# A kernel that orders its own instructions: another charge for TensorE's matmuls in its clock, and some transposes in another order

## The chip, the cores and the metric

The kernel runs on one core of one Trainium2 chip. The metric is the device time of one execution in microseconds, the median over several runs. The names of the engines are those of the profile: PE is TensorE (its matmuls), PEld the loading of its stationary operand, DVE is VectorE, ACT is ScalarE, POOL is GpSimd, SP is SyncE, which issues the weight transfers.

## The reference

The reference is a decoder trunk of two layers over x of 512 positions by 1024 channels, in float32.

```
for l in range(2):
    h = rmsnorm(x)
    p = h @ w_in[l]                          # 1024 -> 3328, split over four mixers
    y = rwkv7(p0), stick_breaking(p1), retention(p2), conformer_conv(p3)   # each 512 x 256
    merged = sum_i sigmoid(h @ w_gate[l, i]) * (y[i] @ w_branch[l, i])
    x = x + merged @ w_out[l]
    h = rmsnorm(x)
    x = x + (swiglu(h) if l == 0 else top2_of_8_experts(h))
```

The RWKV-7 mixer is a recurrence with a 64 x 64 state per head, done here in 8 chunks of 64 positions. The stick-breaking mixer is a causal attention whose logarithms of weights are running sums along the keys. The dense feed-forward part has width 2816. In the last part each of the 512 positions goes to 2 of 8 experts of width 1408.

## The kernel before, in words

**Products.** Every large product is made from three matmuls in the type fp32r: weight and input are each split into a high and a low part, and high x high, high x low and low x high are added up in PSUM. In the trace these are the matmuls that read whi, wlo (two layers) or mhi, mlo, hw (experts). ACT writes the high part of a weight, DVE the low part. The mixers' own small products, and all transposes, are matmuls in float32 (PSUM tile mx, some in po).

**Order.** The program is laid out by Python code that carries a clock of its own (class Clock): for each instruction that is issued it adds a charge to that engine's time, and holds for each stretch of a tile when it will be written and read. The instructions of each engine run in the order in which the code issues them; what the clock says decides nothing but that order. The stream of large matmuls is the backbone. After every six of them (two blocks of three) `group` calls `slot`, and `slot` calls `pump`. `pump` goes through the generators that are under way (rwkv, sb and sb_chunk, ret, conv, norm, moe_put, moe_prep) and lets one go a step further when two conditions hold: its `ready` time is not after PE's time on the clock, and DVE's and ACT's times are not ahead of PE's by more than a limit (LIMS). After a step, `ready` is the time at which all that the step issued will be done, plus 100 ns, or PE's time plus the number of ns that the generator asks for (`yield 6000.0`), whichever is later. So the code puts the small matmuls of a mixer into the backbone where, by its clock, their inputs have been ready for at least 100 ns.

**Charges.** `mm` charges a matmul in fp32r n / 2.4 ns for n columns out (120 ns if n is under 192), one in float32 n / 0.6 ns; `tr` charges a transpose 107 ns. `Engine.cost` charges DVE 69 + 1.042 n and ACT 94 + 0.833 n for most operations. DVE's running sum (tensor_tensor_scan) is charged like any other operation.

**Experts.** The eight expert positions are worked off in the order 4, 0, 5, 1, 6, 2, 3, 7 (PORD). Positions 0 and 1 have room for 160 rows, 2 and 3 for 144, the others for 128 (CAP). While one position is worked, `moe_prep` prepares the next: it builds a one-hot matrix, gathers the rows with an indirect DMA (an index per row), waits 16000 ns of the clock, scales the rows (ACT), waits 6000 ns, then transposes them with PE and splits the result into the tile hw (ACT the high part, DVE the low part). For the larger positions there are two sets of rows: 128, and 32 or 16. For each of the 8 blocks of 128 channels there are then two transposes, one of a 128 x 128 block and one of a 32 x 128 (16 x 128) block. In the trace they are the PE rows of line 478 with mx<-cst,f, with forms 128\*128 128x128 and 32\*128 32x32 (16\*128 16x16).

The lines to know: 473 (the charge in `mm`), 478 (`tr`), 474 (all other matmuls), 214 (all ACT, DVE and POOL operations: `Engine.__getattr__`), 371 (loads of ACT's tables).

Of the kernel before, what the change touches and what calls it, by code (L numbers as in the profile page):

```python
# [10 lines left out]
R = mybir.dt.float32r  # L11
# [8 lines left out]
KC = D // 128  # L20
# [12 lines left out]
CAP = [128 + OV] * 2 + [128 + OV // 2] * 2 + [128] * 4  # L33
# [286 lines left out]
class Trunk:  # L320
# [148 lines left out]
    def mm(self, out, lhsT, rhs, start=True, stop=True):  # L469
        n = 1  # L470
        for d in out.shape[1:]:
            n *= d
        self.clock.run("pe", max(n / 2.4, 120.0 if n < 192 else 27.0) if lhsT.dtype == R else max(n / 0.6, 105.0), [out], [lhsT, rhs])
        self.nc.tensor.matmul(out, lhsT, rhs, start=start, stop=stop)  # L474

    def tr(self, out, in_, ident):
# [31 lines left out]

    def rwkv(self, out):
        m, mm, v, g, a = self.m, self.mm, self.v, self.g, self.a  # L510
        P = self.rwp
        ident, bones = self.c("ident"), self.c("bones")
# [9 lines left out]
        for j in range(2):  # L522
            sl = slice(j * 128, (j + 1) * 128)
            ps = self.ps()
            mm(ps, self.lora[0:64, 0, sl], tw[0:64])
            t = m(S)
            a(t[:], ps, AF.Sigmoid, bias=self.p("w0", j))
            sig.append(t)
            ps = self.ps()
            mm(ps, self.lora[64:128, 0, sl], P[6][64:128])  # L530
            t = m(S)
            a(t[:], ps, AF.Sigmoid, bias=self.p("a0", j))
            aa.append(t)
            if j == 0:
                yield
# [1351 lines left out]
    def moe_prep(self, p, put):  # L1887

        slots = []
        O = self.moe_O(self.moe_new, self.rkp[:, :, p], CAP[p])  # L1890
        yield 5000.0
        self.moe_slots(self.moe_new, O, self.V[:, :, p, :], CAP[p], slots)
        yield 16000.0
        if len(slots) == 1:
            H = [self.mt(n, [128, KC, 128], R) for n in ("hh", "hl")]
            for k0 in (0, 4):
                self.moe_T(slots[0][2][:, k0 * 128:], 4, 128, H[0][:, k0:], H[1][:, k0:])
                yield
        else:
            H = [self.mt("hw", [128, KC, 2, 128 + OV], R, 2)[:, :, :, 0:CAP[p]]]  # L1900
            for _, v, xg, m in slots:
                self.a(xg[0:m], xg[0:m], AF.Identity, scale=v[0:m, 2:3])
            yield 6000.0
            for k0 in range(0, KC, 2):
                ps = self.ps(shape=(128, 2, CAP[p]))
                for k in range(2):
                    for i, (_, _, xg, m) in enumerate(slots):
                        self.tr(ps[:, k, 128 * i:128 * i + m], xg[0:m, (k0 + k) * 128:(k0 + k + 1) * 128],
                                self.c("ident")[0:m, 0:m])
                self.split(H[0][:, k0:k0 + 2, 0], H[0][:, k0:k0 + 2, 1], ps)  # L1910
                if k0 % 4 == 2:
                    yield
        put.append((slots, H))

    def moe_up(self, H, g, r, todo, ks):
# [278 lines left out]
```

## Time and profile before

| | |
|---|---|
| median of 3 runs | 1893.22 us (1893.21 to 1894.51) |
| the profiled execution's own time | 1892.88 us |
| its span, from first to last instruction | 1891.0 us |
| PE busy | 1865.9 us, 99% of the span |
| PEld, DVE, ACT, POOL busy | 1518.9, 1258.0, 970.4, 131.1 us |
| granted TensorE clock | 0.997 of full speed |

Matmuls are pipelined, so that one's duration (say 393 ns) is longer than the distance to the next one's start; what a matmul costs the stream is read from starts. The layers' stages lie so: the first layer's mixers from the start to about 425 us, the dense part to 880 us, the second layer's mixers to about 1360 us, the routing and the first expert's start to 1420 us, the experts to the end.

### The profile page before, as it was taken

What the parts mean: (1) busy time and instruction counts of PE and PEld (TensorE: products, weight loads), DVE (VectorE), ACT (ScalarE), POOL (GpSimd) and SP (SyncE); (2) the same over time, 40 slices, a digit from 0 to 9 for tenths busy, and PEclk for the clock granted to TensorE, in tenths of its full rate; (3) what the DMA queues carried; (4) which work ended last, traced back from release to release, by engine and by line L of the source; (5) the groups of instructions that cost most, each with busy time, mean ns of one, the idle gap of its engine ahead of it and who ended that gap; (6) DMA issues with size and microseconds to landing.
All of it is one profiled execution on the core that took longest, in us unless ns stands there. A gap on an engine that the chain in (4) does not pass through costs nothing. (4 is left out here: it accounts for less than half of the span.)

```text
span 1891.0 us, 26090 instructions
## 1 busy us (share of the span) xinstructions
PE 1865.9 (99%) x10028; PEld 1518.9 (80%) x10028; DVE 1258.0 (67%) x1978; ACT 970.4 (51%) x1427; POOL 131.1 (7%) x184
## 2 busy tenths in 40 slices
PE   8999999999999999999999999999999999999998
PEld 6777777678888888888777877778879889789886
DVE  6779875754663333346778886664578787787776
ACT  5653555743543232235553435674467576676664
POOL 1001100000000000001001100010111011110100
PEclk9999999999999999999999999999999999999999
DMA  5222321132323223224222321133379788798876
GB/s 194 101 79 79 95 79 56 56 128 84 122 101 99 90 101 100 91 91 168 101 78 67 107 89 56 67 118 117 123 303 354 274 320 288 267 346 268 266 247 224
DMA packets 110818, 283.46 MB, mean 150 GB/s; under 512 B 8816, under 2 KB 59632, under 8 KB 102752
## 3 DMA queue, kind: packets, MB, share of 16 engines
q1 hardware_dynamic: 101472, 254.03, 38.5%
q0 software_dynamic: 9072, 27.68, 5.1%
q8 instruction: 81, 1.33, 0.3%
q14 instruction: 49, 0.40, 0.1%
q10 hardware_dynamic: 144, 0.02, 0.0%
HBM read 265.84 MB, written 13.76 MB: 148 GB/s over the span
## 5 line engine op out<-in xcount | busy, mean ns | idle before, releaser
L474 PE MATMUL mm<-s,whi 128*128 128x512 f32 x3168 | 1000.4, 397 | 9.2 <-ACT whi L214 5.8
L474 PEld LDWEIGHTS mm<-s,whi 128*128 128x128 f32 x3168 | 587.4, 188 | 147.4 <-issue 14.2
L474 PE MATMUL mm<-s,wlo 128*128 128x512 f32 x1584 | 619.0, 391 | 0.0
L214 ACT ACTIVATE whi<-wraw 128x512 fp32r<-128x512 f32 (+1 forms) x432 | 261.1, 620 | 212.9 <-PE mm L474 128.1
L214 DVE TENSOR_TENSOR wlo<-wraw,whi 128x512 fp32r<-128x512 f32 (+1 forms) x432 | 286.8, 681 | 123.4 <-ACT whi L214 122.6
L474 PEld LDWEIGHTS mm<-s,wlo 128*128 128x128 f32 x1584 | 298.0, 188 | 64.1 <-DVE wlo L214 0.6
L214 DVE TENSOR_TENSOR mlo<-mraw,mhi 128x2048 fp32r<-128x2048 f32 (+2 forms) x146 | 300.8, 2080 | 25.3 <-ACT mhi L214 25.3
L214 ACT ACTIVATE mhi<-mraw 128x2048 fp32r<-128x2048 f32 (+2 forms) x146 | 253.9, 1750 | 66.8 <-PE po L474 30.6
L214 ACT ACTIVATE s<-s 128x512 f32<-128x512 f32 (+3 forms) x238 | 150.0, 658 | 182.5 <-DVE s L214 180.4
L214 DVE TENSOR_TENSOR s<-s,s 128x512 f32<-128x512 f32 (+19 forms) x369 | 216.2, 593 | 37.4 <-ACT s L214 27.0
L214 ACT ACTIVATE s<-mm 128x512 f32<-128x512 f32 x108 | 64.1, 594 | 214.7 <-PE mm L474 206.5
L214 DVE TENSOR_TENSOR s<-s,mm 128x512 f32<-128x512 f32 x91 | 62.1, 685 | 137.6 <-PE mm L474 111.3
L474 PE MATMUL mm<-mhi,g 128*128 128x512 f32 x352 | 99.5, 393 | 0.0
L474 PEld LDWEIGHTS mm<-mhi,g 128*128 128x128 f32 x352 | 65.4, 188 | 18.4
L214 DVE SCALAR_TENSOR_TENSOR s<-s,par,s 128x512 f32<-128x512 f32 (+31 forms) x110 | 77.5, 733 | 0.4
L474 PE MATMUL mm<-mhi,hh 128*128 128x512 f32 (+1 forms) x192 | 72.4, 377 | 0.0
L474 PE MATMUL mm<-mhi,hl 128*128 128x512 f32 (+1 forms) x192 | 71.5, 372 | 0.0
L214 ACT ACTIVATE s<-mx 128x512 f32<-128x512 f32 (+3 forms) x83 | 39.8, 512 | 54.0 <-PE mx L474 26.5
L474 PE MATMUL mm<-hw,mhi 128*128 128x320 f32 (+1 forms) x384 | 63.8, 306 | 0.0
L474 PEld LDWEIGHTS mx<-s,s 64*64 64x64 f32 (+3 forms) x752 | 41.9, 145 | 21.6 <-issue 13.7
L474 PE MATMUL mm<-mlo,g 128*128 128x512 f32 x176 | 58.7, 392 | 0.0
L371 ACT ACT_TABLE_LOAD x44 | 56.5, 1283 | 0.7
(188 smaller groups left out, 1866.7 us busy)
## 6 DMA issues: line engine op xcount, KB each, us to landing
mraw<-moe_w_d SPq DMA_DIRECT2D x102, 1024.0 KB, 7.0
wraw<-w_gate_d SPq DMA_DIRECT2D x64, 512.0 KB, 3.5
wraw<-ffn_w_d SPq DMA_DIRECT2D x60, 512.0 KB, 3.5
wraw<-w_in_d SPq DMA_DIRECT2D x51, 512.0 KB, 3.5
mraw<-moe_w_d SPq DMA_DIRECT2D x32, 768.0 KB, 6.2
wraw<-w_branch_d SPq DMA_DIRECT2D x32, 256.0 KB, 2.6
mraw<-moe_w_d SPq DMA_DIRECT2D x12, 512.0 KB, 6.0
wraw<-w_out_d SPq DMA_DIRECT2D x10, 512.0 KB, 4.3
```

Of the source, the lines that this page charges most:

```text
L214: return f(out, *a, **k)
L371: self.nc.scalar.preload_act_table_set(want)
L474: self.nc.tensor.matmul(out, lhsT, rhs, start=start, stop=stop)
```

## The change

In `mm` the charge of an fp32r matmul becomes n / 2.4 + 13.7 ns instead of n / 2.4, and the lower bound for n under 192 becomes 109 ns instead of 120. No other charge is touched. For 512 columns that is 227.0 instead of 213.3 ns, for 320 columns 147.0 instead of 133.3, for 288 columns 133.7 instead of 120, for 160 and 144 columns 109 instead of 120.

In `moe_prep`, for the larger positions, the transposes of four channel blocks at a time go into two PSUM tiles: first the four of the 128 rows, then the four of the 32 or 16 rows, and the two splits follow. Before, one PSUM tile held two channel blocks, the two forms took turns, and each tile's split was issued right behind it. There is a `yield` after each four channel blocks, before and after.

```diff
-        self.clock.run("pe", max(n / 2.4, 120.0 if n < 192 else 27.0) if lhsT.dtype == R else max(n / 0.6, 105.0), [out], [lhsT, rhs])
+        self.clock.run("pe", max(n / 2.4 + 13.7, 109.0 if n < 192 else 27.0) if lhsT.dtype == R else max(n / 0.6, 105.0), [out], [lhsT, rhs])
...
-            for k0 in range(0, KC, 2):
-                ps = self.ps(shape=(128, 2, CAP[p]))
-                for k in range(2):
-                    for i, (_, _, xg, m) in enumerate(slots):
-                        self.tr(ps[:, k, 128 * i:128 * i + m], xg[0:m, (k0 + k) * 128:(k0 + k + 1) * 128],
-                                self.c("ident")[0:m, 0:m])
-                self.split(H[0][:, k0:k0 + 2, 0], H[0][:, k0:k0 + 2, 1], ps)
-                if k0 % 4 == 2:
-                    yield
+            for k0 in (0, 4):
+                ps = [self.ps(shape=(128, 2, CAP[p])) for _ in range(2)]
+                for i, (_, _, xg, m) in enumerate(slots):
+                    for k in range(4):
+                        self.tr(ps[k // 2][:, k % 2, 128 * i:128 * i + m],
+                                xg[0:m, (k0 + k) * 128:(k0 + k + 1) * 128], self.c("ident")[0:m, 0:m])
+                for k in (0, 2):
+                    self.split(H[0][:, k0 + k:k0 + k + 2, 0], H[0][:, k0 + k:k0 + k + 2, 1], ps[k // 2])
+                yield
```

## Rows read from the trace of the kernel before

**Rows 1.** The page's first two parts: busy time, share and instructions of each engine, and the granted clock in 40 slices, in tenths.

```profile
PE 1865.9 (99%) x10028; PEld 1518.9 (80%) x10028; DVE 1258.0 (67%) x1978; ACT 970.4 (51%) x1427; POOL 131.1 (7%) x184
...
PEclk9999999999999999999999999999999999999999
```

**Rows 2.** The table of windows, rows for six of the stages: start and end, length, then busy us and instructions of PE, PEld, DVE, ACT, POOL, the granted clock, the DMA engines' share and GB/s.

```profile
15.00:210.00 195.00, 195.00 (x978) 156.23 (x977) 160.91 (x299) 98.05 (x168) 17.39 (x32) 1.00 0.29 96
210.00:425.00 215.00, 209.19 (x1292) 155.50 (x1291) 144.11 (x261) 119.04 (x191) 8.66 (x18) 0.99 0.24 82
425.00:880.00 455.00, 455.00 (x2020) 376.92 (x2019) 212.11 (x338) 162.30 (x276) 11.96 (x28) 1.00 0.31 104
...
1120.00:1310.00 190.00, 188.93 (x1051) 140.79 (x1050) 112.97 (x199) 112.00 (x180) 8.11 (x14) 1.00 0.27 91
1360.00:1420.00 60.00, 57.15 (x338) 48.55 (x337) 41.45 (x90) 34.85 (x39) 10.31 (x11) 1.00 0.74 279
1420.00:1882.00 462.00, 461.73 (x2772) 401.97 (x2771) 354.36 (x386) 305.05 (x343) 44.29 (x24) 1.00 0.85 289
```

**Rows 3.** The waits of PE over the whole span: who waited for whom, us in total, times, the longest. Five of its nine rows; the others are small or lie in the mixers (rows 13).

```profile
PE mm L474 <- ACT whi L214: 5.8, 1, 5.8
...
PE mx L478 <- ACT s L214: 2.4, 4, 0.9
PE mx L474 <- DVE uv L214: 1.4, 2, 0.9
...
PE po L474 <- DVE f L214: 0.8, 1, 0.8
PE mm L474 <- DVE mlo L214: 0.6, 2, 0.4
```

**Rows 4.** The table of windows (columns as in rows 2) for a stretch in the dense part that holds nothing but fp32r matmuls of 512 columns on PE.

```profile
600.00:800.00 200.00, 200.00 (x884) 165.62 (x883) 72.49 (x112) 57.34 (x95) 0.00 (x0) 1.00 0.29 97
```

**Rows 5.** The timeline of PE in an expert with 160 rows (start, length of the run, engine, line, operation, tiles, form of the first, count): eight transposes in turns of the two forms, and the large matmul behind them; then the page's grouping by form of the same eight.

```profile
1549.02 1.75 PE L478 MATMUL mx<-cst,f 128*128 128x128 f32 x8
1550.70 2.12 PE L474 MATMUL mm<-mhi,g 128*128 128x512 f32 x8
...
L478 PE MATMUL mx<-cst,f 128*128 128x128 f32 x4 | 1.3, 314 | 0.0
L478 PE MATMUL mx<-cst,f 32*128 32x32 f32 x4 | 1.0, 244 | 0.0
```

**Rows 6.** The same timeline for a position with 144 rows.

```profile
1672.96 1.70 PE L478 MATMUL mx<-cst,f 128*128 128x128 f32 x8
1674.58 0.73 PE L474 MATMUL mm<-mhi,g 128*128 128x512 f32 x2
```

**Rows 7.** The timeline of PE where eight, and where four, transposes of one form stand together (in the brackets the idle time before).

```profile
379.17 1.09 PE L478 MATMUL mx<-cst,s 128*128 128x128 f32 x8 [0.95 <-ACT s L214]
380.02 0.71 PE L474 MATMUL mm<-s,whi 128*128 128x512 f32 x2
...
1469.65 0.60 PE L478 MATMUL mx<-cst,f 128*128 128x128 f32 x4
1470.00 1.27 PE L474 MATMUL mm<-hw,mhi 128*128 128x320 f32 x7
```

**Rows 8.** The groups by form of PE from 1420 us to the end: all transposes of the small forms in the kernel.

```profile
L478 PE MATMUL mx<-cst,f 32*128 32x32 f32 x16 | 3.9, 244 | 0.0
L478 PE MATMUL mx<-cst,f 16*128 16x16 f32 x16 | 3.7, 231 | 0.0
```

**Rows 9.** The timeline of PE around two other runs of one small form: 64 matmuls with 32 columns in the stationary operand, and 8 with 128 columns in it and 4 columns out.

```profile
225.15 2.11 PE L474 MATMUL mx<-s,f 32*32 32x32 f32 x64
227.19 0.66 PE L478 MATMUL mx<-cst,s 128*128 128x128 f32 x4
...
1452.25 0.95 PE L474 MATMUL mx<-V,O 128*128 128x4 f32 x8
1453.06 1.12 PE L474 MATMUL mm<-hw,mhi 128*128 128x320 f32 x6
```

**Rows 10.** The timeline of DVE and of PE before the transposes of rows 5: the last weights' low parts that DVE made, and the matmuls that read them.

```profile
1541.10 3.42 DVE L214 TENSOR_TENSOR mlo<-mraw,mhi 128x1536 fp32r<-128x1536 f32 x2
...
1551.40 0.88 DVE L214 TENSOR_TENSOR hw<-mx,hw 128x320 fp32r<-128x320 f32 x2
...
1548.33 0.86 PE L474 MATMUL mm<-mlo,hh 128*128 128x384 f32 x4
```

**Rows 11.** The groups by form of DVE from 15 to 1310 us: the running sums.

```profile
L214 DVE TENSOR_TENSOR_SCAN s<-s,s 128x512 f32<-128x512 f32 x12 | 14.2, 1212 | 0.2 <-ACT s L214 0.2
L214 DVE TENSOR_TENSOR_SCAN s<-s,s 128x384 f32<-128x384 f32 x8 | 7.5, 944 | 1.4 <-ACT s L214 1.4
...
L214 DVE TENSOR_TENSOR_SCAN s<-s,s 128x128 f32<-128x128 f32 x8 | 3.2, 400 | 0.0
```

**Rows 12.** The timeline of DVE and of PE around the longest wait of PE in the mixers.

```profile
329.25 2.33 DVE L214 TENSOR_TENSOR_SCAN s<-s,s 128x512 f32<-128x512 f32 x2
331.61 1.83 DVE L214 TENSOR_TENSOR s<-s,s 128x1024 f32<-128x1024 f32 x2
...
335.39 0.68 DVE L214 TENSOR_TENSOR s<-s,mm 128x512 f32<-128x512 f32 x1
...
333.35 0.39 PE L474 MATMUL mm<-s,wlo 128*128 128x512 f32 x1
336.13 0.73 PE L474 MATMUL mm<-s,whi 128*128 128x512 f32 x2 [2.39 <-DVE s L214]
```

**Rows 13.** The waits of PE in the two stages with mixers alone (15 to 440 us, four rows; then 900 to 1360 us, the first of three).

```profile
PE mm L474 <- DVE s L214: 2.4, 1, 2.4
PE mx L478 <- ACT s L214: 2.2, 3, 0.9
PE mx L474 <- ACT s L214: 0.8, 1, 0.8
PE mx L474 <- ACT f L214: 0.4, 1, 0.4
...
PE mm L474 <- DVE s L214: 0.6, 1, 0.6
```

## The prediction

> **What bounds the kernel now.** I read the engines' busy times first. [...] So the stream of matmuls is the bound. The windows by stage tell where it has holes: in the first layer's second half of mixers 209.19 of 215.00 us are busy, in the second layer's 188.93 of 190.00, in the routing 57.15 of 60.00; in the dense part and in the experts nothing is missing but 0.27 us [rows 2]. The list of PE's waits puts names to the holes: 5.8 us are the wait for the first weight, 2.8 us are waits on DVE where the experts' part begins [rows 3], and 5.8 us lie in the first layer's mixers and some 1.0 us in the second's [rows 13], as in the windows. Thus there are two places where a change can gain: cheaper matmuls anywhere in the stream, and at most about 7 us of holes in the mixers. It can lose as much as it opens new holes.
>
> **The transposes.** The trace has 32 transposes of the small forms, 16 of each [rows 8]. Each position with more than 128 rows has 8 of them, which gives the four positions 32; they come in bursts of eight (four large, four small), two bursts a position, so 8 bursts: 4 with 32 rows, 4 with 16. The first kind takes from 1549.02 to the start of the large matmul at 1550.70, 1.68 us [rows 5]; the second 1674.58 - 1672.96 = 1.62 us [rows 6]. Eight transposes of one form take 380.02 - 379.17 = 0.85 us [rows 7]. So taking turns costs 0.83 us a burst (0.77 us with 16 rows), over four changes to the small form and back: 0.21 us (0.19 us) each. After the change there is one such change a burst instead of four. What remains is 0.85 + 0.21 = 1.06 us (1.04 us), what goes is 0.62 us (0.58 us). Over the 8 bursts: 4 x 0.62 + 4 x 0.58 = 4.8 us.
>
> The trace has no run of small transposes of one form, so that part has bounds. The sum takes for each small one 0.85 / 8 = 0.106 us. From below: matmuls with 32 columns in their stationary operand start (227.19 - 225.15) / 64 = 0.032 us apart. From above: nothing is gained in their half at all, and each of the 3 that follow one of its form keeps the 0.18 us that it has now (1.68 / 4 = 0.42 us for a pair, shared as the forms' busy 1.3 and 1.0 us are [rows 5], an estimate). The nearest row is the run of 8 matmuls with 128 columns in the stationary operand and only 4 out, which start (1453.06 - 1452.25) / 8 = 0.10 us apart [rows 9]: the small transposes too have 128 columns there, so I keep 0.106. The bounds for the sum are 4.8 + 24 x 0.074 = 6.6 us and 4.8 - 24 x 0.074 = 3.0 us.
>
> Does the stream get shorter by what the transposes save? Only if nothing else ends the stage. The DMA engines are 0.85 busy from 1420 to 1882 us, DVE for 354 and ACT for 305 of 462 us [rows 2], and none of PE's waits there is on a transfer [rows 3]. DVE finishes the pair of low parts begun at 1541.10 at 1544.52, and the matmuls that use the later of that pair begin at 1548.33, 3.8 us after [rows 10]. PE would have to gain several us on DVE within one expert to catch up; it gains 1.2 us an expert, and the loads go on as buffers come free. The splits of the new order begin behind all eight transposes, not behind the first four, but 0.6 us sooner for the second tile, and hw is read only when the next expert starts. Both tiles come from three PSUM buffers for mx, so the second must be free at the burst's start; each earlier user is done long before. I cost this at nothing; without cover it is one split's 0.44 us (half of the 0.88 us of two [rows 10]) a burst, 3.5 us in all.
>
> [...]
>
> **The charge.** In the dense part 884 matmuls of 512 columns start in 200 us [rows 4]: 226 ns each, where the old clock has 213.3 and the new one 227.0. The old clock was 6% fast against the chip on the backbone, the new one is right within 0.5%. It changes no instruction of the two layers, only the place of generator steps: a step that must wait 4 us of clock time is issued after 17.6 matmuls instead of 18.8. Steps come on average 6% of their wait sooner in the stream. A slot comes every six matmuls, 1.36 us, so a step with a wait of 2 to 4 us (0.12 to 0.24 us sooner) moves to the slot before in some 9 to 18% of cases, and stays where it was in the others. What moves, moves with all that it issues: DVE and ACT operations queue in front of weight splits and of the evacuation of the big products, and its matmuls in front of six others.
>
> [...]
>
> What is such a move worth? DVE and ACT in total have no trouble (161 of 195 us, 144 of 215 [rows 2]). But the charges of DVE are not touched, and one is far off: a running sum over 512 columns is charged 69 + 1.042 x 512 = 602 ns and takes 1212; over 384 columns 469 against 944; over 128, 202 against 400 [rows 11]. A stick-breaking chunk has two to four of them, so its exponentials, and the transposes behind, are 0.7 to 1.3 us later than the clock says. That is where the waits of transposes on ACT come from (2.4 us [rows 3]), and the 2.39 us hole at 336.13: two running sums (2.33 us) and further operations stand in DVE's queue before the evacuation that frees the big product's PSUM [rows 12, 13]. The clock that was fast on PE hid some 0.2 us of this at each place, 6% of about 4 us. There are 12 chunks in the two layers. If each loses all of that cover and waits for it, 12 x 0.24 = 2.9 us are added. On the other side, a mixer that ends sooner can close holes: at most the 7 us. Between a loss of 2.9 us and a gain of 7 us for moves of this size I take 0: the moves are small, most steps stay in their slot, and the holes come from a queue order that can fall either way.
>
> In the experts the charge moves `moe_prep` by at most 10% of its waits of 5, 16 and 6 us, that is 2.7 us of stream; the rows are needed only at the next position, and PE does not wait there now. Routing and the start of the kernel have waits that hang on chains and transfers, not on the place of steps. I take 0 for both.
>
> **Sum.** 1892.9 us for the profiled execution, less 4.8 us: 1888.1. The median of the runs lies 0.3 us higher, which gives 1888.4; I take 1888.2, between them.
>
> **The rivals.** A change under 0.2%, 3.8 us, can't be told from none for this kernel.
>
> A: the forecast, with the mixers' part within 3 us: 1885 to 1891.4. For it: the transposes' saving is read from rows and stands in a stage where PE never waits. Chance 0.55; three in four of it are more than 3.8 us faster.
>
> B: the mixers take the gain back: cover lost at the 12 chunks (2.9 us), and as much at the chain of RWKV's chunks, whose steps go from PE to DVE and back 3 times a chunk, 24 times a layer, 48 in all; at 6% of some 1.3 us each, 0.08 us, 3.7 us. Together 6.6 us against 4.8: 1894.7; with half of it 1891.4. Against it: the old program has only 6.8 us of waits in both mixers [rows 13] although DVE's running sums are misjudged by more than 0.6 us. Chance 0.2, nearly all within 0.2%.
>
> C: the mixers gain: with steps sooner, chains end before their gate, and half to all of the 7 us of holes goes: 1881 to 1884.7. Chance 0.1.
>
> D: the transposes give nothing, since what costs 0.21 us is not the change of form but the small transpose itself: 1892.9. Against it: in the turns even the large one's mean duration grows, 314 ns against the 0.27 us of the last in a run [rows 5, 7]. Chance 0.04.
>
> E: slower. The running sums come to stand in front of evacuations more often. The place is DVE's queue in the gates' part of the mixers, the price is the 2.39 us that one such meeting costs now [rows 12]. Eight chunks of the two layers have running sums of 2.4 us or more in a row (2 x 1212, or 2 x 944 and 2 x 400). Four meetings more cost 9.6 us, less 4.8 is 4.8 us slower, 1897.7; from there on it decides. All eight give 1907. For it: the clock cannot see the sums' true length, and the new order packs steps closer. Against: in the old order one in eight met. Chance 0.11.
>
> **How the numbers follow.** Faster by over 0.2%: three quarters of A (0.41), C (0.1) and a rest of B: 0.52. Slower: E, 0.11. Within 0.2%: 0.37. The range reaches from 1883, which takes in the better bound of the transposes with a small gain in the mixers and the nearer half of C, to 1896, which holds B and D and leaves out most of E.
>
> **What would show it.** The eight bursts at about 1.05 us from their start to the next large matmul, first four of 128\*128, then four of the small form: right; 1.6 us: D. The length from 1420 us on to the last matmul down by 4.8 us. The stages up to 1360 us equal within 3 us, with PE's waits in the mixers near 7 us: A; waits of transposes on ACT at most chunks: B; new holes of over 2 us that wait on DVE, with running sums ahead in its queue: E. The prediction is wrong if the mixers' stages move by more than 4 us either way, or if PE starts to wait for low parts or transfers in the experts.

## The result: 16 us slower, and where they came from

The changed kernel takes 1908.87 us (median of 5 runs, 1906.51 to 1915.63) where the kernel before takes 1893.22; the ratio is 1.0085, interval 1.0071 to 1.0098. Forecast were 1888.2 us and a range of 1883 to 1896. Its profiled execution took 1908.87 us, its span is 1907.0 us. The two views of rows 1 and 2, for the changed kernel:

```profile
PE 1868.9 (98%) x10028; PEld 1523.6 (80%) x10028; DVE 1256.1 (66%) x1977; ACT 956.4 (50%) x1412; POOL 130.7 (7%) x184
```

```profile
15.00:210.00 195.00, 194.69 (x973) 155.40 (x973) 159.26 (x297) 97.49 (x167) 19.06 (x35) 1.00 0.30 94
210.00:425.00 215.00, 206.08 (x1271) 152.95 (x1270) 143.88 (x260) 110.51 (x180) 7.64 (x16) 0.99 0.26 82
425.00:880.00 455.00, 455.00 (x2017) 376.80 (x2016) 210.56 (x333) 162.18 (x276) 8.98 (x20) 1.00 0.32 103
880.00:1120.00 240.00, 238.82 (x1302) 189.76 (x1301) 193.25 (x354) 111.01 (x188) 23.90 (x48) 1.00 0.30 93
1120.00:1310.00 190.00, 182.60 (x1026) 135.64 (x1025) 108.68 (x196) 100.68 (x165) 8.01 (x14) 0.98 0.28 92
1360.00:1420.00 60.00, 58.10 (x349) 51.18 (x348) 31.68 (x76) 27.55 (x40) 9.72 (x13) 0.94 0.49 177
```

The dense part is what it was [rows 2]. In the mixers' windows PE has 8.9 and 7.4 us of holes where it had 5.8 and 1.1, and the granted clock is 0.99 and 0.98 there (before 0.99 and 1.00 [rows 2]) and 0.94 where the routing lies (before 1.00).

Windows of two kernels that drift apart don't hold the same work. But the 7824 large matmuls follow each other in the same order in both, so the time between the starts of the same two of them can be compared. Worked out so from the trace: the first layer from its first large matmul to the last of its gates takes 466.3 us instead of 460.8 (+5.5), the second layer likewise 462.8 instead of 451.0 (+11.8), its output product, where the routing begins, 70.1 instead of 67.6 (+2.5). The dense part is equal, the experts up to the last large matmul take 487.7 instead of 491.8 (-4.1), the end 0.4 more. That is the 16 us.

PE's waits in the two stages with mixers (as rows 13: first 15 to 440 us, then 900 to 1360 us):

```profile
PE mm L474 <- DVE s L214: 4.9, 2, 3.1
PE mx L474 <- ACT s L214: 2.2, 4, 1.4
PE mx L478 <- ACT s L214: 2.1, 3, 1.4
...
PE mx L474 <- ACT s L214: 2.4, 3, 1.6
PE mm L474 <- DVE wlo L214: 1.9, 1, 1.9
PE mx L478 <- ACT s L214: 1.7, 3, 0.7
PE mm L474 <- DVE s L214: 1.1, 1, 1.1
PE mx L474 <- DVE s L214: 1.1, 1, 1.1
PE po L474 <- ACT s L214: 0.3, 1, 0.3
```

They add up to 9.2 + 8.5 = 17.7 us where the kernel before had 6.8 [rows 13]: 10.9 us more. The largest two, in the timelines of DVE, ACT and PE (columns as in rows 12; some lines left out):

```profile
328.01 2.33 DVE L214 TENSOR_TENSOR_SCAN s<-s,s 128x512 f32<-128x512 f32 x2
330.38 1.23 DVE L214 TENSOR_TENSOR s<-s,s 128x1024 f32<-128x1024 f32 x1
331.52 0.68 DVE L214 TENSOR_TENSOR s<-s,mm 128x512 f32<-128x512 f32 x1
...
334.20 0.06 DVE L214 MEMSET eps<- 128x1 f32 x1
337.67 0.69 DVE L214 TENSOR_TENSOR s<-s,mm 128x512 f32<-128x512 f32 x1 [3.41 <-ACT s L214]
...
334.36 0.69 ACT L214 ACTIVATE s<-mx,eps 128x512 f32<-128x512 f32 x1 [1.66 <-DVE eps L214]
335.08 0.63 ACT L214 ACTIVATE s<-s 128x512 f32<-128x512 f32 x1
335.71 1.28 ACT L371 ACT_TABLE_LOAD   x1
337.01 1.67 ACT L214 ACTIVATE s<-s 128x512 f32<-128x512 f32 x3
...
332.26 0.73 PE L474 MATMUL mm<-s,whi 128*128 128x512 f32 x2 [1.76 <-DVE s L214]
338.41 0.73 PE L474 MATMUL mm<-s,whi 128*128 128x512 f32 x2 [3.12 <-DVE s L214]
```

The hole at 332.26 is the meeting of rows 12 again: two running sums and a subtraction stand in DVE's queue before the evacuation that frees the product's PSUM. The hole at 338.41 is the next link: the sums delay a memset of 0.06 us on DVE, ACT's first operation behind it waits for that memset for 1.66 us, then come a table load and the sigmoids, and only then can DVE evacuate.

A part that my sum did not hold at all is the clock. Stretches with a granted clock of 0.50 in the changed kernel up to its last matmul (table of windows, columns as in rows 2):

```profile
316.40:319.80 3.40, 3.40 (x10) 2.62 (x9) 1.91 (x3) 3.31 (x4) 0.00 (x0) 0.50 0.02 5
1214.10:1217.50 3.40, 3.40 (x10) 2.61 (x9) 3.34 (x6) 0.00 (x0) 0.00 (x0) 0.51 0.13 16
1255.10:1258.50 3.40, 3.40 (x10) 2.63 (x9) 0.43 (x1) 2.50 (x5) 0.00 (x0) 0.50 0.00 0
1395.00:1401.80 6.80, 6.70 (x32) 6.74 (x33) 3.31 (x12) 2.84 (x5) 1.50 (x2) 0.50 0.40 135
```

PE is busy in them, at about half the pace: large matmuls start 0.427 us apart there (317.03 to 319.59 us, six steps), in the dense part 0.226. Taken as half, by the granted clock, 17.0 us at 0.50 cost 8.5 us, an estimate. Before three of the falls PE stood idle, 1.44 us to 314.91, 1.88 us to 1212.96, 1.62 us to 1253.80. But holes of 1.76 us (to 332.26), 3.12 us (to 338.41) and 1.41 us (to 374.57) are followed by no fall, and the fourth fall, in the routing, comes with a hole of 0.9 us that the kernel before has too, without a fall. The kernel before has one such stretch of 3.4 us until its last matmul, at 232.8 us, behind small matmuls and a hole of only 0.4 us. By the same estimate the clock makes in these two executions 6.8 us of the difference, 3.4 in the mixers and 3.4 where the routing begins; that the new holes made it fall is not shown. Waits and clock explain 14.3 of the mixers' 17.3 us; the other 3 us are not attributed. In the output product PE waits no longer than before (1.7 us, before 2.2), so its 2.5 us are put down to the clock.

The transposes did what was forecast, and more. One burst of each kind, then the burst of 32 rows by form, as in rows 5 and 6:

```profile
1568.48 0.96 PE L478 MATMUL mx<-cst,f 128*128 128x128 f32 x8
1569.37 0.80 PE L474 MATMUL mm<-mlo,hh 128*128 128x384 f32 x3
...
1690.83 0.95 PE L478 MATMUL mx<-cst,f 128*128 128x128 f32 x8
1691.71 0.61 PE L474 MATMUL mm<-mlo,hh 128*128 128x384 f32 x2
...
L478 PE MATMUL mx<-cst,f 128*128 128x128 f32 x4 | 0.6, 272 | 0.0
L478 PE MATMUL mx<-cst,f 32*128 32x32 f32 x4 | 0.4, 226 | 0.0
```

0.89 us instead of 1.68, and 0.88 instead of 1.62: 4 x 0.79 + 4 x 0.74 = 6.1 us of PE's time.

### The profile page after: what moved, and what is told of

The parts are those of the page before. It is cut to its first block, busy times and chain, and to the rows that moved or that the text cites. A ratio compares the mean times of both kernels' runs of the same rounds, so it can differ in the third digit from the quotient of the medians.

```text
span 1907.0 us, 26077 instructions
## 1 busy us (share of the span) xinstructions
PE 1868.9 (98%) x10028; PEld 1523.6 (80%) x10028; DVE 1256.1 (66%) x1977; ACT 956.4 (50%) x1412; POOL 130.7 (7%) x184
## 5 line engine op out<-in xcount | busy, mean ns | idle before, releaser
L214 DVE TENSOR_TENSOR s<-s,s 128x512 f32<-128x512 f32 (+13 forms) x370 | 217.2, 594 | 44.0 <-ACT s L214 28.7
L214 ACT ACTIVATE s<-s 128x512 f32<-128x512 f32 (+4 forms) x230 | 145.6, 659 | 192.0 <-DVE s L214 188.7
L214 DVE SCALAR_TENSOR_TENSOR s<-s,par,s 128x512 f32<-128x512 f32 (+22 forms) x139 | 95.6, 735 | 0.5
L474 PE MATMUL mx<-s,s 64*64 64x64 f32 (+8 forms) x772 | 60.8, 263 | 4.7 <-ACT s L214 3.5
```

Of the source, the lines that this page charges most:

```text
L214: return f(out, *a, **k)
```

## The experiments

Theory 1: the old charge, 6% too fast, was a cover. It put each step later than the clock's own terms ask for, and so hid that DVE's running sums take twice their charge (1212 ns for 512 columns [rows 11], charged 602). With the true charge for PE alone the steps come too early, and PE waits. Theory 2: any change of a charge deals the order of the instructions anew, and the old order was a good hand. All kernels from here on, other than the second, have the new order of transposes.

**The two edits apart.** First the transposes without the charge, then the charge without the transposes.

```diff
-max(n / 2.4 + 13.7, 109.0 if n < 192 else 27.0)
+max(n / 2.4, 120.0 if n < 192 else 27.0)
```

> The old charge, the transposes in runs by form. All theories: the bursts take 0.88 us instead of 1.65, so some 6 us go, and the mixers are what they were: 1887 us, 0.997 of before. If it is not under 1891, the new order of transposes costs something of its own in the experts.

Measured: 1888.19 us, 0.9969 (0.9955 to 0.9983).

> The new charge, the old transposes. If the two edits simply add, the mixers lose their 17 to 20 us as in the changed kernel and the experts keep the slow bursts: 1913 to 1916 us, 1.011. If it stays under 1905, the loss needs both edits together.

Measured: 1911.87 us, 1.0088 (1.0072 to 1.0105), a little under the range for edits that simply add. The transposes give 5 to 6 us with the old charge and 3.0 with the new one, the charge costs 18 to 21: the loss is the charge's, and the two add within 3 us. In this kernel all of ACT's and DVE's instructions stand in the same order as in the changed kernel, and PE's but for the transposes.

**The running sums charged as measured, and half of the charge.** The first adds to the changed kernel (its lines are numbered two higher from there on):

```diff
+        if name == "tensor_tensor_scan":
+            return 145.0 + 2.115 * n
```

> The changed kernel, and DVE's running sums charged 145 + 2.115 n ns (1228 for 512 columns, as measured) instead of 69 + 1.042 n. Theory 1 (a true PE charge takes away the cover for DVE operations that are charged too little, the running sums first): most of the 17 us in the mixers come back, 1888 to 1895 us. Theory 2 (any other set of charges deals the order of steps anew, and the old one was a good hand): a new order again, anywhere from 1890 to 1910, with other waits in other places.

Measured: 1885.88 us, 0.9952 (0.9937 to 0.9967): all that the charge had cost is back, and 2.3 us more than the transposes alone give. Theory 1 expected 1888 at best, theory 2 1890. Its waits of PE in the two stages with mixers:

```profile
PE mx L480 <- ACT s L216: 1.4, 1, 1.4
PE mm L476 <- DVE s L216: 0.7, 1, 0.7
...
PE mm L476 <- ACT whi L216: 1.3, 1, 1.3
PE mm L476 <- DVE s L216: 0.6, 2, 0.4
```

4.0 us instead of 17.7, and less than before the change (6.8).

> The changed kernel with half the added charge (n / 2.4 + 6.85 ns, lower bound 114.5). Theory 1: half the cover is gone, so about half of the loss: 1897 us. Theory 2: not in between but anywhere, 1885 to 1912.

Measured: 1891.06 us, 0.9981 (0.9971 to 0.9990). With the half charge the loss is 2.9 of 20.7 us, not half as theory 1 expected (1897 us). Neither theory is ruled out by these four.

**Neighbours of the new charge, and other ways to put steps later.** The running sums as measured beside the old PE charge; 400 ns of slack instead of 100 (`SLACK = (400.0, 400.0)`); and 1 ns more or less in the new charge:

```diff
-max(n / 2.4 + 13.7, 109.0 if n < 192 else 27.0)
+max(n / 2.4 + 14.7, 109.0 if n < 192 else 27.0)
```

> The old PE charge, the new order of transposes, the running sums charged as measured. Theory 1 (steps too early for late DVE work are what costs): steps behind running sums come later than in the kernel with the transposes alone (1888.2), so no worse, 1883 to 1889. Theory 2 (each set of charges deals a new hand): anywhere from 1885 to 1910.

Measured: 1890.46 us, 0.9984 (0.9974 to 0.9993), a little above what theory 1 expected.

> The changed kernel with 400 ns instead of 100 ns added to each step's ready time; all charges as in the changed kernel. Theory 1: the cover comes back in another way, 0.3 us a step where the old charge gave 0.1 to 0.25, so most of the loss goes: 1888 to 1898 us. Theory 2: anywhere from 1885 to 1912.

Measured: 1895.49 us, 1.0007 (0.9997 to 1.0017).

> The changed kernel with 14.7 ns instead of 13.7 ns added: 1 ns in 227, of no meaning for when work is ready. Theory 1: the time of the changed kernel, 1909, within 5 us. Theory 2: the order is dealt anew by so small a change, and the time moves by more than 5 us, more likely down than up.

> The changed kernel with 12.7 ns instead of 13.7 ns added. Theory 1: within 5 us of 1909, a little below. Theory 2: off by more than 5 us, more likely down than up.

Measured: 1896.59 us, 1.0015 (1.0005 to 1.0024), and 1896.22 us, 1.0016 (1.0006 to 1.0025). One ns of 227, either way, takes 12 us off. Theory 2 holds to that extent: the new charge is a bad hand among its neighbours. What 14.7 ns spares is the clock and the longest holes: it has 3.4 us at a granted clock of 0.50 before its end instead of 17.0 (6.8 us), and waits in the mixers of 13.6 instead of 17.7 us. Its first stage's waits:

```profile
PE mx L478 <- ACT s L214: 2.4, 4, 1.2
PE mm L474 <- DVE s L214: 1.7, 1, 1.7
PE mx L474 <- ACT s L214: 1.1, 2, 0.9
```

With 12.7 ns it is another part: the clock is no better there (20.5 us at 0.50 before the end), but PE waits 11.6 us in the mixers, and the second layer takes 452.6 instead of 462.8 us. But both neighbours are still 8 us above the kernel with the transposes alone.

**Neighbours of the old charge, and of the true clock.** 1 ns more and less than n / 2.4; 14.7 and 12.7 ns beside true running sums.

> The kernel with the transposes alone, 1 ns added to the old charge of fp32r matmuls. Theory 1 (a level set by the PE charge): 1888 within 3 us. Theory 2 (scatter alone, the old charge a good hand): 1888 to 1900, as the two neighbours of the new charge lay 12 us below it. Both together: a scatter of some 5 us around a level under that of the new charge.

> The same with 1 ns taken from the old charge. Theory 1: 1888 within 3 us. Theory 2: 1888 to 1900.

Measured: 1885.36 us, 0.9955 (0.9939 to 0.9971), and 1894.55 us, 1.0002 (0.9993 to 1.0012). The old charge has neighbours on both sides, 9 us apart; it was no rare hand.

> The kernel with the new charge and the running sums charged as measured, with 14.7 ns instead of 13.7 ns. Theory 1: 1886 within 4 us, since the clock is true for both. Theory 2: 1886 was a good hand, this one lies at 1888 to 1900.

> The same with 12.7 ns. Theory 1: 1886 within 4 us. Theory 2: 1888 to 1900.

Measured: 1888.95 us, 0.9979 (0.9969 to 0.9989), and 1885.04 us, 0.9948 (0.9928 to 0.9968), the fastest of all.

**Level and scatter.** A draw is here one order of the instructions, as one set of charges deals it; a family is the draws with nearly the same charges. Two more draws of each of two families, the new charge with the old and with true running sums, then two more amounts of slack.

> The changed kernel with 11.7 ns instead of 13.7 ns. Both theories together (a level set by how late DVE's uncharged work is against the steps, and a scatter of some 5 us from the hand dealt): near 1896 to 1900, above the 1885 to 1895 of the old charge. Theory 2 alone: as likely under 1890 as over it.

> The changed kernel with 15.7 ns. Both: 1894 to 1904. Theory 2 alone: as likely under 1890 as over it.

> The running sums charged as measured and 11.7 ns: both theories together 1884 to 1890, with the first layer's gates in 276 us as in the three draws before. Theory 2 alone: 1885 to 1900.

> The running sums charged as measured and 15.7 ns: both theories together 1884 to 1890, the first layer's gates in 276 us. Theory 2 alone: 1885 to 1900.

> The changed kernel with 300 ns of slack. If any later step will do in place of a true charge: 1885 to 1890. If it must be the steps behind the running sums: 1893 to 1902, as with 400 ns.

> The changed kernel with 500 ns of slack. If any later step will do: 1885 to 1890. If it must be the steps behind the running sums: 1892 to 1900.

Measured medians, then from the profiled executions the mixers' time, from a layer's first large matmul to the last of its gates (worked out from the trace as above), and the sum of PE's waits from 15 to 440 us:

| charge of a large matmul, ns over n / 2.4 | us | first layer, us | second layer, us | waits in the first layer, us |
|---|---|---|---|---|
| -1 | 1894.6 | 461.4 | 455.4 | 4.6 |
| 0 (old) | 1888.2 | 460.6 | 451.0 | 5.8 |
| +1 | 1885.4 | 458.4 | 451.0 | 4.9 |
| +6.85 | 1891.1 | 462.0 | 451.8 | 7.2 |
| +11.7 | 1896.6 | 465.7 | 452.7 | 8.1 |
| +12.7 | 1896.2 | 465.2 | 452.6 | 7.8 |
| +13.7 (the change) | 1908.9 | 466.3 | 462.8 | 9.2 |
| +14.7 | 1896.6 | 461.8 | 457.4 | 6.5 |
| +15.7 | 1895.1 | 465.8 | 453.4 | 8.8 |
| 0, true running sums | 1890.5 | 456.8 | 456.9 | 2.6 |
| +11.7, true running sums | 1887.2 | 454.5 | 454.5 | 2.0 |
| +12.7, true running sums | 1885.0 | 455.5 | 455.0 | 2.0 |
| +13.7, true running sums | 1885.9 | 455.5 | 453.5 | 2.1 |
| +14.7, true running sums | 1889.0 | 455.6 | 458.0 | 2.9 |
| +15.7, true running sums | 1889.9 | 460.1 | 454.5 | 3.4 |
| +13.7, slack 300 | 1892.0 | 457.3 | 458.0 | 4.6 |
| +13.7, slack 400 | 1895.5 | 459.9 | 456.7 | 4.0 |
| +13.7, slack 500 | 1896.7 | 460.9 | 456.1 | 7.3 |

The five draws about the new charge lie at 1895 to 1909, the five with true running sums at 1885 to 1890: the ranges don't touch. So the level is real, 9 us between the medians (1896.6 and 1887.2). The scatter within a family is 5 us with true running sums, and 1.5 us with the new charge without the one bad draw. The three draws of the old charge lie 9 us apart, and the slowest (1894.6) all but meets the new charge's fastest (1895.1): that the old charge's level is the lower one rests on less. The draws with 11.7 and 15.7 ns came as both theories together expected; 300 ns of slack (1892.0) lies between its two expectations, 500 ns in the second. The level lies in the first layer, where the middle draw of the old charge takes 460.6 us, of the new one 465.7, of the new one with true running sums 455.5. There the level is one of PE's waits: 6.5 to 9.2 us with the new charge, 4.6 to 5.8 with the old one, 2.0 to 3.4 with true running sums beside the new charge, and 2.6 beside the old. Between the middles of the new charge and of true running sums the waits make 6 of the 10 us. And they are longer at the place that theory 1 names: most transposes that wait for ACT stand behind a chunk's running sums. Their waits with the new charge, 15 to 1310 us, for 11.7 to 15.7 ns in order:

```profile
PE mx L478 <- ACT s L214: 5.7, 6, 1.9
PE mx L478 <- ACT s L214: 4.8, 5, 1.2
PE mx L478 <- ACT s L214: 3.8, 6, 1.4
PE mx L478 <- ACT s L214: 4.6, 7, 1.6
PE mx L478 <- ACT s L214: 2.0, 1, 2.0
```

The old charge has 0.4 to 2.4 us of them, true running sums none in two draws and at most 1.9. The time at a granted clock of 0.50 does not part the families: up to the last matmul it is 3.4 to 20.5 us with the new charge and 0 to 13.7 with true running sums.

In the second layer the order of the families is another: 451.0, 453.4, 454.5. Later steps cost a little there. Slack shows both: it brings the first layer down to 457 to 461 us, and takes the second up to 456 to 458. A delay of all steps is thus no substitute for a true charge of the few that are late. Whether a higher charge for another operation of DVE would do as much as the running sums' was not tried. The forecast of 276 us for the first layer's gates with true running sums held for 11.7 (275.4 us) and not for 15.7 (279.8).

The changed kernel's 11.8 us in the second layer are not the family's: its four neighbours take 452.6 to 457.4 us there. By the medians, then, the 16 us are made of 5.0 that the transposes give, 8.4 that the new charge's level costs against the transposes alone, and 12.3 by which this draw lies above its family's middle.

## Why the prediction was wrong

**Right: the bound and the transposes.** PE's stream bounds the kernel (busy for 99% of the span before [rows 1], for 98% now), and a cheaper stream passes through to the end: the transposes alone gave a ratio of 0.9969, 5.9 us at 1893.2. The term of 4.8 us was too small by 1.3 on PE, most of it for the small transposes: by the trace they start 0.062 us apart (an estimate of 0.106 stood there, bounds 0.032 and 0.18). Rival D is out.

**Right: the charge itself.** The new kernel's dense part has 884 matmuls in 200 us as before [rows 4], so 226 ns is the period. Draws with charges from 11.7 to 15.7 beside true running sums lie at 1885 to 1890, so the charge is not what was wrong.

**Wrong: the step "between a loss of 2.9 us and a gain of 7 us I take 0".** Measured are 17.3 us in the mixers and 2.5 in the output product. Three things failed in it. First, "the moves are small, most steps stay in their slot": each step that moves moves all later ones. Of the 1558 small matmuls of the two layers that can be paired by name and shape between the kernel with the transposes alone and the changed one, 1404 stand behind another number of large matmuls; 1 ns more on the charge moves 1482 of 1862. The order is a new one, with its own holes. Nor do the steps come "on average 6% of their wait sooner in the stream": on average 832 large matmuls stand before a small one of the first layer, where it was 826, and the families overlap in this (807 to 839 with the new charge, 811 to 848 with true running sums). That steps come too early is thus shown only against the running sums, by the waits, and not as a shift of all steps. Second, the price of the lost cover: 12 chunks x 0.24 us = 2.9 us was a size too small. The family's middle draw is 8.4 us above the transposes alone, 5.1 of them in the first layer's mixers. The cause named for it was right, the running sums at twice their charge: charging them truly, and nothing else, brings the first layer to 455.5 us. (By the trace a column more costs (1212 - 944) / 128 = 2.1 ns in a running sum [rows 11], and (1223 - 689) / 512 = 1.0 ns in a TENSOR_TENSOR, with 1223 and 689 ns for 1024 and 512 columns in the kernel before, 15 to 1310 us.) The bound counted only what each chunk's own transposes wait, and left out that what is late in DVE's queue holds up ACT, the evacuations and the weights' low parts behind it, as the chain from 328.01 to 338.41 us shows. Third, the clock: the sum had no term for it. The 9 of each slice [rows 1] does not show such stretches, since a 9 is 90% or more of 47 us: the kernel before already had 3.4 us at a granted clock of 0.50. Three new holes of 1.4 to 1.9 us were each followed by 3.4 us at 0.50, which adds 1.7 us by the same estimate, about the hole's own length; others of that length were followed by none.

**Rival E was the nearest.** It forecast 1897.7 us for four more meetings of running sums and evacuations and 1907 for eight, at a chance of 0.11. Its mechanism is there: at 332.26 us (1.76 us, the meeting of rows 12 again), behind it at 338.41 (3.12 us), and at 1198.48 (1.14 us). But not all holes are of its kind: at 314.91 and 1253.80 us (1.44 and 1.62 us) PE waits for ACT, whose long operations on 1024 columns (three in 3.3 us, from 310.04 and from 1249.93 us) stand before the copies that free a chunk's PSUM. Of the bad draw's excess over its neighbour with 14.7 ns, 13.2 us in the profiled spans, the clock makes 6.8 by the same estimate, the mixers' waits 4.1. The range ended at 1896, which four of the five draws of the new charge exceed by 0.6 us at most or stay under: they lie between B (1894.7, whose sign, transposes that wait for ACT, they show in part) and E's four meetings (1897.7). B and E together should have had more than 0.31, since the profile showed which error the change uncovered, and 0.6 us of misjudgement a sum is six times the slack of a step. That this draw came out 12 us above its neighbours, beyond even E's 1907, is chance, which neither the forecast nor a rival held.

**In the experts** "nothing else ends the stage" held but for one hole of 1.89 us at 1464.19, where ACT's scaling of a result stood behind a weight split that waited 3.31 us for its transfer. The kernel with the charge alone, whose transposes are slow, has none; 14.7 ns has 0.6 us there.

## What to carry to other kernels

A planner with several wrong charges works by their balance: correcting one alone can be worse than correcting none, because it uncovers another wrong one, here a running sum that takes twice its charge. Where an order is made by such a planner, a single variant says little: charge a little more and a little less, and compare the families' middles, before a change is kept or dropped. Grouping the transposes by form shortened each burst by the same 0.7 to 0.8 us with either charge; of these 6.1 us the kernel kept 5 to 6 with the old charge and 3.0 with the new.

The fastest here, true charges for both PE and the running sums (12.7 ns: 1885.04 us, 0.9948, interval 0.9928 to 0.9968), beats both kernels; that it beats the old charge plus 1 ns (1885.36) can't be said.

## What the runs showed of the hardware

Two equal holes need not have equal consequences for the clock. The changed kernel's longest hole, 3.12 us to 338.41, is followed by no fall. The kernel with the charge alone has the same order there and the same hole, and its clock falls for 6.8 us (table of windows, then PE's row):

```profile
337.10:343.90 6.80, 5.63 (x40) 4.38 (x41) 6.27 (x10) 4.04 (x8) 0.00 (x0) 0.50 0.23 77
...
338.27 1.22 PE L474 MATMUL mm<-s,whi 128*128 128x512 f32 x2 [3.14 <-DVE s L214]
```

Nor is the clock the same in every execution of one kernel. The five of the changed kernel took 1906.51, 1906.99, 1908.87, 1911.22 and 1915.63 us, at granted clocks of 0.993, 0.994, 0.994, 0.991 and 0.990: their spread of 9.1 us (the kernel before 4.5) goes with the clock, as 0.004 of 1907 us are 7.6 us. What decides whether a hole is followed by a fall stays open.

A change of form cost more here than a small transpose: within its run one of 32 rows starts 0.062 us after the other, and one of 128 rows 0.108 us (the changed kernel's burst at 1568.48 us); eight in one run of each form take 0.89 us, 0.21 more than these spacings add up to, and in turns 1.68 us [rows 5], 1.00 more, which is 0.25 us for each change from 128 rows to 32 and back.
